# Weight sums issued in the recurrent stage, remainder sums in an earlier phase, the last output pair in pieces

## The chip, the cores and the metric

The kernel runs on one core of a Trainium2 chip. The metric is the device time of one execution, in microseconds (us). The core has a matrix engine (TensorE, PE in the profile), VectorE (DVE), ScalarE (ACT), GpSimd (POOL), and SyncE (SP), which only issues transfers here. POOL issues transfers too. All of them are carried out by the same 16 DMA engines. Each engine works through its instructions in order.

## The reference, cut to what matters

One layer of a streaming encoder, in float32, for 1024 prompt tokens and 32 sample tokens (1056 columns in all), width 1024:

```python
h = rms_norm(x, g_pre_mix)
z = h @ w_in                       # q_A k_A v_A | q_B f_B i_B og_B | gates
ya = sink_attention(...)           # A: 16 heads, window of chunks of 64
yb = hgrn2(...)                    # B: gated linear recurrence, 8 heads of 128
yb = rms_norm(yb) * silu(og_B)
mix = sigmoid(ga) * (ya @ w_br_a) + sigmoid(gb) * (yb @ w_br_b)
x = x + rms_norm(mix @ w_out, g_post_mix)
a, u = split(rms_norm(x) @ w_up)   # 2 x 2816
a = causal_depthwise_conv3(a)
x = x + rms_norm((gelu(a) * u) @ w_down)
x = x + (pe @ w_ple) * sigmoid(x @ w_ple_gate)
```

Beside the tokens it returns the last keys and values, the recurrent state and the last rows ahead of the convolution.

## The kernel before, in words

Every product is made in three: weights and activations are split into a high and a low part, and `product` (L201, L202, L203) multiplies high by high, low by high and high by low. For the large products the kernel uses a Strassen-like scheme with seven block products in place of eight; that needs sums of weight blocks and sums of activation blocks, and sums of the seven results afterwards.

The stages follow one another on PE: the transposed and normed input and attention (A) up to about 402 us; the recurrent stage (B), eight heads; the branches and the output product; the up product; from about 1640 us the down product, in three parts (`seg`) of two phases (`ph`) each; at last the gates and the output.

**Sums of w_down.** The down product needs sums of blocks of `w_down`, for four of its seven products. They are made without an engine: eight sums (`w_sums`), each in four columns, are 32 transfers from DRAM to the DRAM scratch `w_d`, issued by POOL (L1441). 24 read `w_down` and eight read another sum; the transfers that add use the accumulating form. In the program they are traced in the recurrent stage, one every five pieces of work (`at(8 + 5 * (4 * n + c), w_sum)`).

**What sets the order.** A scheduler of the framework places the traced instructions on each engine, and may move one ahead of others traced before it if nothing binds it. `behind(engines)` names the last traced instruction of each of these engines and binds what is traced inside the `with` to come after it; this acts on an instruction of the same engine. The sums are bound to nothing in the kernel before.

**The start.** Input tiles are loaded, transposed and stored to `xt_d` through four buffers `xc` (L775 copies on ACT, L776 stores by SP). Weight columns are loaded to `wr` by SP (L171), and split by ACT (L180, high part `wh`) and DVE (L182, low part `wl`). L339 writes keys into place, L294 stores gates to `ta_d` and `tb_d`. Attention weights `sc` are scaled on DVE (L510) and transposed on PE (L533).

**The recurrent stage.** For each head POOL fills a few tiles, copies `ke` (L1294) and loads the state `S` of the sample (L1315), which DVE uses at L1338. `TL` (L978) and `wu` (L1018) are loads by SP.

**The down product.** `d_unit` runs the products of a column pair `c`, and DVE adds each product's result into accumulators `acc` or into the temporaries `S` and `T`. `rest(c)` (L2251 on) subtracts `S` from `T` (L2255), and adds or subtracts the remainder in three accumulators (L2222). All four calls stand in the second phase of the last part.

**The end.** `gate_one(q, c)` makes the gate product of a quarter `q` and a column pair `c` (both columns `a`) and `y_out` applies tanh and adds; `late_y` turns finished pages back to rows by transposes (L2514, L2526), copies them (L2519, L2520, L2527) and stores them (L2507, L2509, L2531).

Of the kernel before, what the change touches and what calls it, by code (L numbers as in the profile page):

```python
# [10 lines left out]
F32 = mybir.dt.float32  # L11
F32R = mybir.dt.float32r
I32 = mybir.dt.int32
AF = mybir.ActivationFunctionType
ALU = mybir.AluOpType
AX = mybir.AxisListType

P = 128
D = 1024
KT = 8  # L20
# [10 lines left out]
H = 264  # L31
# [28 lines left out]
def layer_kernel(  # L60
# [10 lines left out]
    wp = ctx.enter_context(tc.tile_pool(name="wp", bufs=1, side="left"))  # L71
# [6 lines left out]
    def nm(s):  # L78
        n_names[0] += 1
        return f"{s}_{n_names[0]}"  # L80
# [4 lines left out]
    dma, gdma = nc.sync.dma_start, nc.gpsimd.dma_start  # L85
    V, S, G, E = nc.vector, nc.scalar, nc.gpsimd, nc.tensor

    def behind(*engines):

        st = ExitStack()  # L90
        for e in engines:
            ins = next(i for i in reversed(nc.cur_bb.bb.instructions) if i.engine == e.engine)
            st.enter_context(tc.issue_after(ins))
        return st


    ident = cp.tile([P, P], F32, name="ident")
# [30 lines left out]
    w_d = {o: dp.tile([P, 4, NF // 2, P], F32, name=f"w_d{o}") for o in (1, 3, 4, 6)}  # L128
# [22 lines left out]
    for i in range(8):  # L151
        done, q = sum(G_AT[:i]), [("q", i + 1)] * (3 if i < 7 else 0)
# [86 lines left out]
    def tr_bank():  # L239
        return bank(pp, "tr", 2)  # L240
# [72 lines left out]
    with right("ap") as ap:  # L313
# [91 lines left out]
        qs, biases, yas, probs, o8 = {}, {}, {}, {}, {}  # L405
# [189 lines left out]
        with tc.tile_pool(name="np", bufs=1, side="right", reuse_waits="tile") as np_:  # L595
# [121 lines left out]
            rows = vector_rows()  # L717
# [208 lines left out]
        for i in range(8):  # L926
            lo_ = 2 * len(blocks) if i else 0
            q = unit(q_out(i + 1)) if i < 7 else []
# [148 lines left out]
    with right("bp") as bp:  # L1077
# [309 lines left out]
        pieces, small = [], {}  # L1387
# [49 lines left out]
        for n, (o, a, h, other) in enumerate(w_sums):  # L1437
            for c in range(4):
                def w_sum(o=o, src=w_d[other][:, c] if other else dv[:, a, h, c], c=c,
                          op={"accum_op": ALU.add} if n > 3 else {}):  # L1440
                    gdma(w_d[o][:, c], src, **op)  # L1441
                at(8 + 5 * (4 * n + c), w_sum)
        for m, (run, ev) in enumerate(pieces):
            run()
# [32 lines left out]
    with right("mp") as mp:  # L1477
# [33 lines left out]
        for b_, (c, g) in enumerate(order):  # L1511
            if c == len(ws):
                ws.append(next_w())
            o, n = G4[g]
            ta = mt("ta", 4)
            dma(ta[:], ta_d[c][:, o:o + n])
            b = block(ws[c], ALL, Ra[g], Rb[g], KS, n)
# [25 lines left out]
        for c in range(8):  # L1543
# [3 lines left out]
            for g, (o, n) in enumerate(G4):  # L1547
# [4 lines left out]
                b = block(w, ALL, Ya[g], Yb[g], KS, n)  # L1552
# [321 lines left out]
    for p in range(2):  # L1874
        for c in range(8):
# [14 lines left out]
            if c == 1:  # L1890
# [3 lines left out]
                op0 = build_ops(0)  # L1894
# [16 lines left out]
    t = tr_bank()  # L1911
# [11 lines left out]
    def rows(p):  # L1923
        for h in range(2):
            o, a = H * (2 * p + h), 6 * (1 - p) + 3 * h
            norm_rows(rs[:, a:a + 3], T88, rbT[:, o:o + H])
# [277 lines left out]
    def st_bank():  # L2204
        return pf.tile([P, 2, 512], F32, tag="st", name=nm("st"), bufs=3)
# [45 lines left out]
    def rest(c):  # L2251

        acc = acc_t[c]
        r = S_[:, c]
        V.tensor_tensor(r, T1_[:, c], r, op=ALU.subtract)  # L2255
        add(acc[:, 1], r, ALU.subtract)
        add(acc[:, 3], r)
        add(acc[:, 2], r)
# [26 lines left out]
    def phase_step(pt, ph, s):  # L2285


        if ph == 0:
            a, z_ = range(8), 3
            ops_ = [(pt, 3 + n // 2, n % 2) for n in range(8)]  # L2290
        elif pt < 2:
            a, z_ = range(6), 4
            ops_ = [(pt + 1, n // 2, n % 2) for n in range(6)]
        else:
            return
        if s < len(ops_):
            q, i, p = ops_[s]
            load_op(q, p, i)
        m = s - z_
        if ph:  # L2300
            m = m // 2 if m >= 0 and m % 2 == 0 else -1
        if 0 <= m < len(ops_):
            q, i, p = ops_[m]
            split_ops(q, i, (p,))

    for seg in range(3):
        for ph in range(2):
            if seg == 2 and ph == 1:
                break
            for c in range(4):  # L2310
                def beside(n, c=c):
                    phase_step(seg, ph, len(OPS[ph]) * c + n)
                    if (seg, ph) == (0, 0) and n == 1 and c < 2:
                        with behind(V):
                            next(last_sums)
                d_unit(seg, ph, c, beside=beside)
# [82 lines left out]
    def y_small(n):  # L2399
        return xs_page[0][:, 3].rearrange("p a c -> p (a c)")[:, 256 * (n % 2):256 * (n % 2) + 256]  # L2400
# [3 lines left out]
    for c in range(2):  # L2404
        def beside(n, c=c):
            if n == 0:
                with behind(V):
                    rest(c)
            if n == 1:
                square(c, 0)  # L2410
            if n == 2:
                with behind(S, V):
                    gate_parts(2 * c)
            if n == 3 and c == 0:
                with behind(S, V):
                    gate_parts(1)
        d_unit(2, 1, c, beside=beside)

    def beside(n):
        if n == 0:  # L2420
            with behind(V):
                rest(2)
        if n == 1:
            square(2, 0)
        if n == 2:
            with behind(V):
                rest(3)
        if n == 3:
            square(3, 0)
            xs_page.append(ep.tile([P, 4, 2, H], F32, tag="T1", name="xs"))  # L2430
            for c in range(3):
                x1_load(0, c)
# [27 lines left out]

    d_unit(2, 1, 2, (1,), w2, beside)

    def gate_mults(q, c, b, ks):
        for a in range(2):
            product(b[:, a, :H], gw[2 * c + a], ALL, [xh[q][:, k] for k in range(KT)],
                    [xl[q][:, k] for k in range(KT)], [(k, k) for k in ks], ks[0] == 0, ks[-1] == KT - 1)

    ys, n_pl, n_y = {}, [0], [0]

    def y_out(q, c, b):  # L2470

        p, h = divmod(q, 2)
        if h == 0:
            if not y_pg:
                y_pg.append(page_at(wb_[0], [P, 2, 2, 2 * H], "y").bitcast(F32))
            ys[p, c] = y_pg[0][:, n_y[0] % 2]
            n_y[0] += 1
        y = ys[p, c][:, :, H * h:H * h + H]
        pl = misc[0][:, 2 + n_pl[0] % 2]
        n_pl[0] += 1  # L2480
        dma(pl, ple_d[:, 2 * c:2 * c + 2, H * q:H * q + H])
        ak = columns(q, c)
        for a in (slice(0, 2),) if (q, c) != (3, 3) else (slice(0, 1), slice(1, 2)):
            S.activation(y[:, a], b[:, a, :H], AF.Tanh, scale=0.5)
            V.scalar_tensor_tensor(y[:, a], y[:, a], 1.0, pl[:, a], op0=ALU.add, op1=ALU.mult)
            V.scalar_tensor_tensor(y[:, a], y[:, a], 0.5, ak[:, a], op0=ALU.mult, op1=ALU.add)

    y_pg = []
    TY = (((0, P), (P, P), (2 * P, P), (3 * P, P), (4 * P, 16)),
# [3 lines left out]
    def y_done(p, c):  # L2493

        y = ys.pop((p, c))
        o = 2 * H * p
        fin = (p, c) == (1, 3)
        yr = wp.tile([P, 4, 2 * P], F32, tag="wr", name=nm("yr"), bufs=2)
        sm = y_small(n_done[0])
        n_done[0] += 1  # L2500
        r = TY[p][4][1]
        m3 = TY[p][3][1]

        def rows(z_):
            f = slice(2 * c * P + z_.start, 2 * c * P + z_.stop)
            n = 4 if m3 == P else 3
            dma(y_prompt[0, o:o + n * P, f].rearrange("(a p) c -> p a c", p=P), yr[:, 0:n, z_])  # L2507
            if n == 3:
                dma(y_prompt[0, o + 3 * P:o + 3 * P + m3, f], yr[:m3, 3, z_])  # L2509

        for a in range(2):
            t = tr_bank()
            for i, (c_, m_) in enumerate(TY[p][:4]):
                E.transpose(t[:m_, i * P:(i + 1) * P], y[:, a, c_:c_ + m_], ident[:])  # L2514
            z_ = slice(a * P, (a + 1) * P)
            if m3 == P:
                S.copy(yr[:, :, z_], t[:].rearrange("p (a b) -> p a b", b=P))
            else:
                S.copy(yr[:, 0:3, z_], t[:, :3 * P].rearrange("p (a b) -> p a b", b=P))  # L2519
                S.copy(yr[:m3, 3, z_], t[:m3, 3 * P:])  # L2520
            if fin:
                rows(z_)
        t = tr_bank()
        c_, _ = TY[p][4]
        for a in range(2):
            E.transpose(t[:r, a * P:(a + 1) * P], y[:, a, c_:c_ + r], ident[:])  # L2526
        S.copy(sm[:r], t[:r, :2 * P])  # L2527
        if not fin:
            rows(slice(0, 2 * P))
        f = slice(2 * c * P, (2 * c + 2) * P)  # L2530
        dma(y_sample[0, :, f] if p else y_prompt[0, o + 512:o + 528, f], sm[:r])  # L2531

# [2 lines left out]
    def late_y(n):  # L2535
        while len(late) > n:
            y_done(*late.pop(0))
# [10 lines left out]
    def gate_one(q, c):  # L2548
        b = st_bank()
        gate_mults(q, c, b, tuple(range(KT)))  # L2550
        if q % 2 == 0 or c == 3:
            late_y(1 if q != 3 else 0)
        y_out(q, c, b)
        if q % 2:
            late.append((q // 2, c))
# [25 lines left out]
    for m, (q, c) in enumerate(((0, 2), (1, 2), (0, 3), (1, 3))):  # L2581
        gate_one(q, c)
        for kp in range(2):
            x2_pair(2 + m // 2, 2 * (m % 2) + kp)
    for c in range(4):
        for q in (2, 3):
            gate_one(q, c)
    late_y(0)
    qctx.close()


# [30 lines left out]
```

## Time and profile before

| | us |
|---|---|
| median of 3 runs | 2035.63 (2035.2 to 2039.28) |
| the profiled execution | 2033.22 |
| its span | 2031.4 |
| PE busy | 1951.6 (96%) |
| DVE busy | 1433.0 (71%) |
| ACT busy | 997.8 (49%) |
| POOL busy | 300.7 (15%) |
| mean granted TensorE clock | 0.984 |

In a row of a group the profile gives the source line, the engine, the operation, output and input by the program's names, how often it occurs, and durations. In a row of the timeline stand the start, the duration, the same names, and in square brackets the idle time of the engine ahead of it and what ended that. A row with `SPq` is an issue on SP's queue: its duration is that of the issue, not of the transfer. In a row of windows stand, for each engine, the busy time in that stretch and the number of instructions; then the granted clock (1.00 is full), the mean busy share of the 16 DMA engines (above 1 where more transfers are under way than engines) and what they moved in GB/s.

### The profile page before, as it was taken

What the parts mean: (1) busy time and instruction counts of PE and PEld (TensorE: products, weight loads), DVE (VectorE), ACT (ScalarE), POOL (GpSimd) and SP (SyncE); (2) the same over time, 40 slices, a digit from 0 to 9 for tenths busy, and PEclk for the clock granted to TensorE, in tenths of its full rate; (3) what the DMA queues carried; (4) which work ended last, traced back from release to release, by engine and by line L of the source; (5) the groups of instructions that cost most, each with busy time, mean ns of one, the idle gap of its engine ahead of it and who ended that gap; (6) DMA issues with size and microseconds to landing.
All of it is one profiled execution on the core that took longest, in us unless ns stands there. A gap on an engine that the chain in (4) does not pass through costs nothing. (4 is left out here: it accounts for less than half of the span.)

```text
span 2031.4 us, 38387 instructions
## 1 busy us (share of the span) xinstructions
PE 1951.6 (96%) x14715; PEld 1930.4 (95%) x14715; DVE 1433.0 (71%) x3170; ACT 997.8 (49%) x2181; POOL 300.7 (15%) x423
## 2 busy tenths in 40 slices
PE   5668999999999999999999999999999999999998
PEld 4568999999999999999999999999999999999998
DVE  3346777778888888855355588878787787667872
ACT  4335777766665666645123475333333335534332
POOL 5041212000000000001200123243434320000000
PEclk8789999999999999999999999999999999999999
DMA  9995435231112111148666775333333338555343
GB/s 317 256 204 132 131 90 150 63 131 45 55 57 78 57 54 57 57 139 250 201 187 193 233 242 185 101 106 107 106 107 106 106 113 283 188 182 175 111 128 93
DMA packets 296317, 283.12 MB, mean 139 GB/s; under 512 B 14853, under 2 KB 266376, under 8 KB 296133
## 3 DMA queue, kind: packets, MB, share of 16 engines
q1 hardware_dynamic: 270437, 224.86, 35.7%
q0 software_dynamic: 25696, 55.80, 10.7%
q8 instruction: 116, 1.90, 0.4%
q14 instruction: 68, 0.56, 0.1%
HBM read 195.46 MB, written 100.28 MB: 146 GB/s over the span
## 5 line engine op out<-in xcount | busy, mean ns | idle before, releaser
L2098 PE MATMUL st<-op,wt 128*128 128x264 f32 x1232 | 348.9, 283 | 3.2 <-ACT Sp L2109 1.4
L2100 PE MATMUL st<-op,wt 128*128 128x264 f32 x1232 | 349.7, 284 | 0.0
L2099 PE MATMUL st<-op,wt 128*128 128x264 f32 x1232 | 347.6, 282 | 0.0
L2098 PEld LDWEIGHTS st<-op,wt 128*128 128x128 f32 x1232 | 231.2, 188 | 5.0 <-ACT Sp L2109 2.1
L2099 PEld LDWEIGHTS st<-op,wt 128*128 128x128 f32 x1232 | 231.4, 188 | 0.0
L2100 PEld LDWEIGHTS st<-op,wt 128*128 128x128 f32 x1232 | 230.8, 187 | 0.0
L2217 PE MATMUL st<-dop,wt 128*128 128x264 f32 x616 | 174.8, 284 | 3.3 <-DVE acc L2222 1.9
L2219 PE MATMUL st<-dop,wt 128*128 128x264 f32 x616 | 174.3, 283 | 0.0
L2218 PE MATMUL st<-dop,wt 128*128 128x264 f32 x616 | 174.0, 282 | 0.0
L1762 ACT CAST wt<-wu 128x512 fp32r<-128x512 f32 x126 | 75.9, 618 | 178.1 <-POOL ab L2084 75.5
L201 PE MATMUL mm<-La,wh 128*128 128x384 f32 (+1 forms) x480 | 161.3, 336 | 0.0
L202 PE MATMUL mm<-Lb,wh 128*128 128x384 f32 (+1 forms) x480 | 158.2, 330 | 0.7 <-DVE Lb L771 0.4
L203 PE MATMUL mm<-La,wl 128*128 128x384 f32 (+1 forms) x480 | 157.4, 328 | 0.1
L201 PE MATMUL mm<-Ra,wh 128*128 128x264 f32 x512 | 145.4, 284 | 0.0
L202 PE MATMUL mm<-Rb,wh 128*128 128x264 f32 x512 | 145.0, 283 | 0.0
L203 PE MATMUL mm<-Ra,wl 128*128 128x264 f32 x512 | 145.0, 283 | 0.0
L2217 PEld LDWEIGHTS st<-dop,wt 128*128 128x128 f32 x616 | 115.7, 188 | 4.4 <-ACT wg L2336 1.8
L1763 DVE TENSOR_TENSOR wt<-wu,wt 128x512 fp32r<-128x512 f32 x126 | 86.4, 694 | 46.7 <-ACT wt L1762 46.7
L2218 PEld LDWEIGHTS st<-dop,wt 128*128 128x128 f32 x616 | 115.7, 188 | 0.0
L2219 PEld LDWEIGHTS st<-dop,wt 128*128 128x128 f32 x616 | 115.4, 188 | 0.0
L180 ACT CAST wh<-wr 128x1024 fp32r<-128x1024 f32 x51 | 53.4, 1048 | 97.5 <-PE mm L202 54.1
L202 PEld LDWEIGHTS mm<-Rb,wh 128*128 128x128 f32 x512 | 96.5, 188 | 0.0
(569 smaller groups left out, 6073.8 us busy)
## 6 DMA issues: line engine op xcount, KB each, us to landing
wu<-in_w_up_dram SPq DMA_DIRECT2D x42, 512.0 KB
wu<-in_w_in_dram SPq DMA_DIRECT2D x36, 512.0 KB
w_d<-in_w_down_dram POOLq DMA_DIRECT2D x24, 704.0 KB, 21.3
a_d<-Up SPq DMA_DIRECT2D x22, 528.0 KB
wr<-in_w_in_dram SPq DMA_DIRECT2D x21, 512.0 KB
s_d<-sm SPq DMA_DIRECT2D x40, 264.0 KB
dop<-s_d SPq DMA_DIRECT2D x16, 528.0 KB
wr<-in_w_out_dram SPq DMA_DIRECT2D x16, 512.0 KB
```

The costliest lines, as they stand in the source:

```text
L180: S.copy(hi[:], raw[:])
L201: E.matmul(ps, wh, a, start=first and n == 0, stop=False)
L202: E.matmul(ps, wh, b, start=False, stop=False)
L203: E.matmul(ps, wl, a, start=False, stop=last and n == len(ks) - 1)
L1762: S.copy(t[:, 0], src)
L1763: V.tensor_tensor(t[:, 1], src, t[:, 0].bitcast(F32), op=ALU.subtract)
L2098: E.matmul(o, wh, xh, start=first and k == 0, stop=False, skip_group_check=True)
L2099: E.matmul(o, wh, xl, start=False, stop=False, skip_group_check=True)
L2100: E.matmul(o, wl, xh, start=False, stop=k == 3, skip_group_check=True)
L2217: E.matmul(o, wh, xh_, start=first and k == 0, stop=False, skip_group_check=True)
L2218: E.matmul(o, wh, xl_, start=False, stop=False, skip_group_check=True)
L2219: E.matmul(o, wl, xh_, start=False, stop=k == ng - 1, skip_group_check=True)
```

## The change

There are three edits. First, the 32 transfers of the sums are traced inside `with behind(E, V, G)`. Second, `rest(0)` and `rest(1)` are called in the first phase of the last part (columns 2 and 3, second product), and `rest(2)` and `rest(3)` in the second phase at columns 0 and 1. Third, the last output pair (quarter 3, columns 3) is made in pieces: the two columns' products apart, the first two tiles of the page turned and stored between them, the other three tiles per column, the last column's tanh in pieces of 120 and 144, one copy on DVE, and one store issued by ACT.

```diff
                 def w_sum(o=o, src=w_d[other][:, c] if other else dv[:, a, h, c], c=c,
                           op={"accum_op": ALU.add} if n > 3 else {}):
-                    gdma(w_d[o][:, c], src, **op)
+                    with behind(E, V, G):
+                        gdma(w_d[o][:, c], src, **op)
                 at(8 + 5 * (4 * n + c), w_sum)
...
                 def beside(n, c=c):
                     phase_step(seg, ph, len(OPS[ph]) * c + n)
+                    if (seg, ph, n) == (2, 0, 1) and c > 1:
+                        with behind(V):
+                            rest(c - 2)
...
             if n == 0:
                 with behind(V):
-                    rest(c)
+                    rest(c + 2)
...
     def beside(n):
-        if n == 0:
-            with behind(V):
-                rest(2)
         if n == 1:
             square(2, 0)
-        if n == 2:
-            with behind(V):
-                rest(3)
...
-        if q % 2 == 0 or c == 3:
-            late_y(1 if q != 3 else 0)
+        if q % 2 == 0:
+            late_y(1 if (q, c) != (2, 3) else 0)
...
-    for c in range(4):
-        for q in (2, 3):
-            gate_one(q, c)
-    late_y(0)
+    for q, c in ((2, 0), (3, 0), (2, 1), (3, 1), (2, 2), (3, 2), (2, 3)):
+        gate_one(q, c)
+
+    b = st_bank()
+    ks = tuple(range(KT))
+    gate_mults(3, 3, b, ks, (0,))
+    y = ys[1, 3]
+    yr = wp.tile([P, 4, 2 * P], F32, tag="wr", name=nm("yr"), bufs=2)
+    t = tr_bank()
+    for i in range(2):
+        for a in range(2):
+            o = (2 * i + a) * P
+            E.transpose(t[:, o:o + P], y[:, a, i * P:(i + 1) * P], ident[:])
+    S.copy(yr[:, 0:2].rearrange("p a c -> p (a c)"), t[:])
+    o = 2 * H
+    dma(y_prompt[0, o:o + 2 * P, 6 * P:8 * P].rearrange("(a p) c -> p a c", p=P), yr[:, 0:2])
+    one = slice(0, 1), slice(0, H)
+    piece = y_out(3, 3, b, (one,))
+    gate_mults(3, 3, b, ks, (1,))
...
+    t = tr_bank()
+    for i in (2, 3, 4):
+        last_turn(0, t, i)
+    for i in (2, 3, 4):
+        last_rows(0, t, i, dma)
+    z1, z2 = slice(0, 3 * P - H), slice(3 * P - H, H)
+    t = tr_bank()
+    piece(slice(1, 2), z1)
+    last_turn(1, t, 2)
+    piece(slice(1, 2), z2)
+    last_turn(1, t, 3)
+    last_turn(1, t, 4)
+    for i, q in ((2, dma), (3, S.dma_start), (4, dma)):
+        last_rows(1, t, i, q)
```

In the program as it is placed on the engines, POOL's instructions near the start of the kernel before are these (`w_d_...` are the scratch tensors of the sums, `K...` the keys, `x...` an input tile):

```order
L694 AFFINE_SELECT cm<-cm 128x128
L699 DMA nsink<-in_attn_sinks_dram 128x16
L1441 DMA w_d_144<-in_w_down_dram 128x11x128
L718 COPY tb_185<-tb 32x128
L1441 DMA w_d_144<-in_w_down_dram 128x11x128 x3
L601 MEMSET x_435 32x1024
L602 MEMSET x_435 64x1024
L1441 DMA w_d_145<-in_w_down_dram 128x11x128 x4
L1441 DMA w_d_143<-in_w_down_dram 128x11x128 x4
L1441 DMA w_d_146<-in_w_down_dram 128x11x128 x4
L413 MEMSET qa_1011 128x64
```

None of the sums stands there in the changed kernel. Its first ones on POOL come after the first fills of the recurrent stage, and the others among the heads' instructions:

```order
L1087 MEMSET resets 128x6
L1090 MEMSET z_4929 128x128
L1442 DMA w_d_144<-in_w_down_dram 128x11x128 x2
L1245 MEMSET tq_5027 128x96
L1442 DMA w_d_144<-in_w_down_dram 128x11x128 x2
L1442 DMA w_d_145<-in_w_down_dram 128x11x128
L1245 MEMSET d_933_5325 128x96
L1294 COPY ke_5326<-vt_5242 128x32
L1245 MEMSET tq_5521 128x96
L1442 DMA w_d_145<-in_w_down_dram 128x11x128
L1442 DMA w_d_143<-in_w_down_dram 128x11x128
L1302 MEMSET kk_5633 32x128
```

So the sums moved past all of POOL's attention work. In the last heads the sums that read another sum stand ahead of a head's state load:

```order
L1442 DMA w_d_143<-w_d_145 128x1408
L1442 DMA w_d_146<-w_d_143 128x1408
L1302 MEMSET kk_8522 32x128
L1303 MEMSET kk_8522 64x128
L1442 DMA w_d_143<-w_d_145 128x1408
L1315 DMA S_8741<-in_state_hgrn_dram 128x128
L1442 DMA w_d_143<-w_d_145 128x1408
L1245 MEMSET d_1534_8887 128x96
L1294 COPY ke_8888<-vt_8768 128x32
```

There the load of `S` and the copy `ke` now have sums ahead of them. On DVE, in the last part of the down product, `rest` (the subtraction into `S` and three additions with `S`) stands in the second phase in the kernel before, between the additions of that phase's results `st`:

```order
L2222 TENSOR_TENSOR acc_20038<-acc_20038,st_22222 128x528
L2255 TENSOR_TENSOR S_20039<-T_20035,S_20039 128x528
L2222 TENSOR_TENSOR sq_22081<-sq_22081 128x528
L2222 TENSOR_TENSOR acc_20038<-acc_20038,S_20039 128x528 x3
L2222 TENSOR_TENSOR acc_20038<-acc_20038,st_22223 128x528
L1870 TENSOR_TENSOR wt_22328<-wd_22256,wt_22328 128x512
```

In the changed kernel two of the four groups stand in the first phase, where DVE also prepares operands (`dop`) and weights (`wt`):

```order
L2223 TENSOR_TENSOR T_20035<-T_20035,st_21886 128x528
L2073 TENSOR_TENSOR dop_21846<-dop_21846 128x1056
L2256 TENSOR_TENSOR S_20039<-T_20035,S_20039 128x528
L1871 TENSOR_TENSOR wt_22023<-wd_21919,wt_22023 128x512
L2223 TENSOR_TENSOR acc_20037<-acc_20037,S_20039 128x528 x3
L2223 TENSOR_TENSOR acc_20036<-acc_20036,st_21885 128x528
L2073 TENSOR_TENSOR dop_21881<-dop_21881 128x1056
```

So these two groups moved ahead of the second phase altogether. The other two now follow the first results of its first two columns.

More of the change, by code (lines that the diff above doesn't have):

```diff
@@ L2461, in layer_kernel, with gate_mults @@
     d_unit(2, 1, 2, (1,), w2, beside)
-    def gate_mults(q, c, b, ks):
-        for a in range(2):
+    def gate_mults(q, c, b, ks, cols=range(2)):
+        for a in cols:
             product(b[:, a, :H], gw[2 * c + a], ALL, [xh[q][:, k] for k in range(KT)],
@@ L2468, in layer_kernel, with y_out @@
     ys, n_pl, n_y = {}, [0], [0]
-    def y_out(q, c, b):
+    def y_out(q, c, b, pieces=((slice(0, 2), slice(0, H)),)):
         p, h = divmod(q, 2)
@@ L2482, in y_out, with piece @@
         ak = columns(q, c)
[L2483 to L2486, printed above, removed]
+        def piece(a, z_):
+            S.activation(y[:, a, z_], b[:, a, z_], AF.Tanh, scale=0.5)
+            V.scalar_tensor_tensor(y[:, a, z_], y[:, a, z_], 1.0, pl[:, a, z_], op0=ALU.add, op1=ALU.mult)
+            V.scalar_tensor_tensor(y[:, a, z_], y[:, a, z_], 0.5, ak[:, a, z_], op0=ALU.mult, op1=ALU.add)
+        for z_ in pieces:
+            piece(*z_)
+        return piece
     y_pg = []
@@ L2496, in y_done @@
         o = 2 * H * p
-        fin = (p, c) == (1, 3)
         yr = wp.tile([P, 4, 2 * P], F32, tag="wr", name=nm("yr"), bufs=2)
@@ L2520, in y_done @@
                 S.copy(yr[:m3, 3, z_], t[:m3, 3 * P:])
-            if fin:
-                rows(z_)
         t = tr_bank()
@@ L2527, in y_done @@
         S.copy(sm[:r], t[:r, :2 * P])
-        if not fin:
-            rows(slice(0, 2 * P))
+        rows(slice(0, 2 * P))
         f = slice(2 * c * P, (2 * c + 2) * P)
@@ L2584, in layer_kernel, with last_rows, last_turn @@
             x2_pair(2 + m // 2, 2 * (m % 2) + kp)
-    for c in range(4):
-        for q in (2, 3):
-            gate_one(q, c)
-    late_y(0)
+    for q, c in ((2, 0), (3, 0), (2, 1), (3, 1), (2, 2), (3, 2), (2, 3)):
[16 more added lines that the diff above has]
+    gate_mults(3, 3, b, ks, (1,))
+    sm = y_small(n_done[0])
+    def last_rows(a, t, i, qs):
+        c_, m_ = TY[1][i]
+        z_, f = slice(a * P, (a + 1) * P), slice((6 + a) * P, (7 + a) * P)
+        if i < 4:
+            (V.tensor_copy if i == 3 else S.copy)(yr[:m_, i, z_], t[:m_, i * P - 2 * P:i * P - P])
+            qs(y_prompt[0, o + c_:o + c_ + m_, f], yr[:m_, i, z_])
+        else:
+            S.copy(sm[:m_, z_], t[:m_, 2 * P:3 * P])
+            qs(y_sample[0, :, f], sm[:m_, z_])
+    def last_turn(a, t, i):
+        c_, m_ = TY[1][i]
+        E.transpose(t[:m_, i * P - 2 * P:i * P - P], y[:, a, c_:c_ + m_], ident[:])
+    t = tr_bank()
[12 more added lines that the diff above has]
+        last_rows(1, t, i, q)
     qctx.close()
```

## The prediction

> **What bounds the kernel now.** I read the slices of the span first, then a table of windows over the start, then the waits there, and last single rows.
>
> ```profile
> PE   5668999999999999999999999999999999999998
> DMA  9995435231112111148666775333333338555343
> ```
>
> Each digit is a fortieth of the span, some 51 us. TensorE (PE) is full from the fifth slice to the last one, so what can be won in the middle is small. It is not full in the first four, and there the DMA engines are. The table of windows cuts these four into stretches.
>
> ```profile
> core 0: us, PE busy (x) PEld busy (x) DVE busy (x) ACT busy (x) POOL busy (x), PEclk, DMA share, GB/s
> 0.00:26.00 26.00, 21.57 (x111) 19.03 (x112) 14.57 (x31) 17.10 (x31) 18.61 (x33) 1.00 0.97 333
> 26.00:67.00 41.00, 10.33 (x37) 8.49 (x35) 4.24 (x10) 5.66 (x12) 14.26 (x12) 0.58 1.05 296
> 67.00:108.00 41.00, 35.60 (x218) 33.01 (x218) 24.78 (x66) 22.18 (x46) 8.26 (x17) 0.92 0.91 220
> 108.00:172.00 64.00, 39.49 (x240) 36.93 (x239) 26.17 (x75) 21.88 (x65) 16.27 (x26) 0.84 1.16 218
> 172.00:400.00 228.00, 227.38 (x1598) 225.36 (x1596) 171.59 (x560) 168.38 (x463) 36.83 (x111) 1.00 0.38 104
> ```
>
> From 172 us on, PE idles 0.6 us in 228. Before that it idles 4.4 + 30.7 + 5.4 + 24.5 = 65.0 us, and no other engine is nearly full either: DVE is busy 24.78 of 41 us at most. Only the DMA share stands at 0.91 to 1.16. Whose transfers these are, the rows of the sums' destination `w_d` tell (number, nanoseconds each at least, in the middle and at most, first and last start).
>
> ```profile
> L1441 POOL DMA_DIRECT2D w_d<-in_w_down_dram x24: 1049/1055/3485, 10.5 to 112.8; - x24
> L1441 POOL DMA_DIRECT2D w_d<-w_d x8: 802/812/845, 124.7 to 155.1; - x8
> L1858 SPq DMA_DIRECT2D wd<-w_d x48: 320/430/1227, 1645.8 to 1880.6; - x48
> DMA to landing us min/median/max: 7.7/18.3/42.2
> w_d<-in_w_down_dram POOLq DMA_DIRECT2D x24, 704.0 KB, 21.3
> ```
>
> All 32 are issued by 155.1 us, though nothing reads them before 1645.8. At 704 KB each they are 23.1 MB. The windows moved 8.7 + 12.1 + 9.0 + 14.0 = 43.8 MB up to 172 us, so the sums are half of it. The waits of that stretch (total, times, longest, in us) and the rows of the long ones:
>
> ```profile
> ACT xc L775 <- DMA xt_d<-xc: 36.3, 4, 17.6
> ACT wh L180 <- DMA wr<-in_w_in_dram: 29.2, 2, 22.1
> 47.06 1.65 PE L302 MATMUL tr<-ident,n 128*128 128x128 f32 x6 [14.38 <-ACT xc L775]
> 64.47 0.90 PE L644 MATMUL tr<-ident,x 128*128 128x128 f32 x3 [13.85 <-ACT xc L775]
> 128.41 2.12 SPq L171 DMA_DIRECT2D wr<-in_w_in_dram  x2
> 130.62 19.54 SPq L294 DMA_DIRECT2D ta_d<-gt  x1
> 153.72 1.04 ACT L180 CAST wh<-wr 128x1024 fp32r<-128x1024 f32 x1 [22.09 <-DMA wr<-in_w_in_dram]
> 156.64 1.14 PE L533 MATMUL tr<-ident,sc 128*128 128x128 f32 x4 [19.45 <-DVE sc L510]
> ```
>
> Twice ACT cannot fill a buffer `xc` because its store to `xt_d` has not left, and PE behind it stands 14.38 and 13.85 us. Once a weight load issued at 128.41 is there only at 153.72, 25 us later, and ACT, DVE and PE wait in turn (19.45 us of PE). The SP row of 19.54 us is one issue: SP's queue is held up as well. These transfers stand in one pool with the sums.
>
> **The change part by part, A: the sums.** Their order on POOL moves from the start to behind the first fills of the recurrent stage, which begins near 402 us; PE, DVE, ACT and SP keep their order up to the last part of the down product. Gone from the start are 23.1 MB, 24 issues of 1.05 us at the least and eight of 0.81. What remains there is 20.7 MB. If the 172 us shrink to 117, that is 177 GB/s, against the 333 that the first window reached; so the rest need not bound the start.
>
> The gain, stretch by stretch. In 26 to 67, the idle time is 30.7 us, of which the two `xc` waits are 28.2. The clock was 0.58 there:
>
> ```profile
> 26.12 0.33 PE L202 MATMUL mm<-Lb,wh 128*128 128x384 f32 x1
> 48.82 0.52 PE L202 MATMUL mm<-Lb,wh 128*128 128x384 f32 x1
> ```
>
> The same matmul took 0.52 us behind the wait and 0.33 ahead of it; without the idle time 10.33 us of work become 6.6, 3.8 us less. I take 29 of these 34.5 us, since a store must still leave its buffer. In 67 to 108 I take 4 of the 5.4 idle. In 108 to 172 the 19.45 are due to the late load; the rest of that stretch's idle time is 5.1 us, most of it in pieces that belong to the attention's own chain, and the clock of 0.84 costs some 2 us more. I take 21. Of the first window, 1. Sum: 29 + 4 + 21 + 1 = 55 us. Bounds: at the most everything, 65 + 3.8 + 2 = 70; at the least half of it, 28, if other transfers take the place of the sums, as below.
>
> What the sums cost in their new place. The rows there:
>
> ```profile
> 400.00:500.00 100.00, 99.17 (x654) 98.16 (x654) 79.28 (x169) 61.61 (x132) 2.03 (x11) 1.00 0.29 94
> 500.00:550.00 50.00, 50.00 (x339) 49.82 (x338) 42.88 (x127) 31.26 (x86) 1.65 (x6) 1.00 0.19 58
> 700.00:750.00 50.00, 50.00 (x337) 49.84 (x337) 42.12 (x117) 33.84 (x91) 1.36 (x5) 1.00 0.15 41
> 465.04 0.36 POOL L1294 COPY ke<-vt 128x32 f32<-128x32 f32 x1 [62.05 <-DVE d L1248]
> 504.49 0.57 POOL L1315 DMA_DIRECT2D S<-in_state_hgrn_dram  x1 [21.11 <-PE so L1360]
> 508.48 0.33 DVE L1338 SCALAR_TENSOR_TENSOR S<-S,dec,so 128x128 f32<-128x128 f32 x1
> 418.82 2.78 SPq L978 DMA_DIRECT2D TL<-t_d  x4
> ```
>
> POOL is busy 2 us in 50 and idles 62 us at a stretch, and the DMA share is 0.15 to 0.29: 23.1 MB over some 350 us add 66 GB/s to 41 to 94. PE, though, is full, so what is late there costs directly. Queued behind the sums on POOL are the copy `ke`, two fills and the state's load `S` of each head. `S` is used 4.0 us after its issue. A sum right ahead of it puts it back by an issue (1.05 us) and by its share of the transfer (704 KB at 333 GB/s are 2.2 us), together 3.3 us, which just fits. The first five sums, 3.6 MB or 10.8 us, are issued from 402 and are through near 413, ahead of the four `TL` loads at 418.82. I take a cost of 2 us; bounds 0 (all of it fits) and 16 (eight heads, 2 us each).
>
> A rule stands against this place. The Trainium skill, page "SBUF — State Buffer", section "SBUF: two separate sides", says that a DMA issued by GpSimd has its descriptors written by GpSimd, which some VectorE operations lock out, so the transfer starves. No row of before shows it. By the rule alone each issue would be longer in a stage with DVE at 0.85; even at the longest issue of a sum above (3.49 us) POOL's idle time holds all 32, so my sum stays.
>
> **B: the remainder sums.** Four groups of DVE work move from the second phase of the down product's last part; two of them into its first phase, and the other two from the third column to the first two columns.
>
> ```profile
> 1850.00:1880.00 30.00, 30.00 (x250) 30.00 (x250) 24.77 (x33) 12.14 (x18) 0.00 (x0) 1.00 0.41 123
> 1880.00:1910.00 30.00, 28.01 (x230) 27.29 (x229) 27.08 (x51) 11.95 (x21) 0.00 (x0) 1.00 0.39 116
> 1898.71 0.70 DVE L2255 TENSOR_TENSOR S<-T,S 128x528 f32<-128x528 f32 x1
> 1899.68 1.94 DVE L2222 TENSOR_TENSOR acc<-acc,S 128x528 f32<-128x528 f32 x3
> 1902.72 0.36 PE L2217 MATMUL st<-dop,wt 128*128 128x264 f32 x1 [1.63 <-DVE acc L2222]
> ```
>
> One group is 0.70 + 1.94 = 2.6 us. PE idles 2.0 us in 1880 to 1910, 1.63 of it behind such a group. In the first phase DVE has 5.2 us free in 30, and PE none: two groups, 5.3 us, just fit there. I take a gain of 1.5; bounds 2.0, and a loss of 1.5 if the first phase has DVE late by half of what moves.
>
> **C: the last output pair.** Rows of PE and SP at the end:
>
> ```profile
> 2023.03 0.28 PE L203 MATMUL st<-xh,wg 128*128 128x264 f32 x1
> 2023.15 1.04 PE L2514 MATMUL tr<-ident,y 128*128 128x128 f32 x8
> 2025.15 1.09 PE L2514 MATMUL tr<-ident,y 128*128 128x128 f32 x8 [0.15 <-ACT yr L2520]
> 2028.67 0.39 SPq L2531 DMA_DIRECT2D out_dram<-xs  x1
> ```
>
> Today PE's last product ends at 2023.3; 20 transposes, the copies and eight stores follow, and the span ends at 2031.4, 2.7 us after the last issue. In the change 14 of these transposes (ten of the page before the last, four of the last) stand ahead of the last column's products. A group of eight is 1.04 us; so 14 put the last product back by 1.8 us, to 2025.1. Behind it come six transposes, and shorter pieces: tanh, two DVE operations, a transpose, a copy and the last issue, which I put near 2028.2. Gain 0.5 us; bounds +1 and -1.5 (all of the 1.8 kept but for 0.3).
>
> **The sum.** 55 - 2 + 1.5 + 0.5 = 55 us. The profiled execution took 2033.22 us (span 2031.4 and 1.8 around it) and would take 2033.2 - 55 = 1978.2. The median of the runs, 2035.63, lies 2.4 above it, so I forecast 1980.6. Its own range: 28 to 70 us of A make 1966 to 2008.
>
> **The rivals.**
>
> *The start has a second limit.* Half of the bytes stay, and so does the chain load, split, product; SP still issues one transfer after another, and a store may hold `xc` for long anyway. For it: the first window moved 333 GB/s with PE at 21.57 of 26. Against it: the two rows of `xc` are at 296 GB/s, when sums were most of what flowed. Price: 28 in place of 55, so 2035.6 - 28 = 2007.6. Chance 0.12.
>
> *The recurrent stage gives some back.* `S`, `TL` or `wu` come late behind bursts. It decides where a wait is over the 4.0 us that `S` has. Price: 16 in place of 2: 1994.6. For it: PE has no idle time there. Against it: a DMA share of 0.15 to 0.29. Chance 0.08.
>
> *The wait isn't the sums'.* If each queue of transfers had its share of the engines whatever the other holds, SP's load of 512 KB would be through in twice its 1.6 us at 333 GB/s, not in 25; then the 25 are SP's own queue's (19.54 us for one issue), and the start stays. Left are B and C: 2035.6 - 2.0 = 2033.6, within 0.2%. Against it: SP's own bytes alone can't fill a share of 1.16. Chance 0.03. The Trainium skill, page "DMA: Bandwidth & Descriptors", section "Queues, rings and completion order", has this rule: each DMA engine takes the queues that hold work in turn, a packet at a time. The 25 us of the trace don't look like an even share of bytes.
>
> *Slower: POOL's queue stalls each head.* A sum that waits for a sum (the last eight do: `w_d<-w_d` follow each other every 4.3 us on the mean, and one transfer in the middle lands after 18.3 us) holds the copy `ke` and the load `S` behind it, and PE with them. It decides where a head loses over 57 / 8 = 7.1 us; at 18.3 us less the 4.0 us of slack for each of eight heads it is 114, and 2035.6 - 57 + 114 = 2093. Against it: only in the last two heads do such sums stand ahead of `S`; those ahead of the others read the weights alone. Chance 0.03.
>
> **How the numbers follow.** What a measurement of this kernel can tell from no change is 0.2%, 4 us. The forecast has 0.74, the rivals 0.12, 0.08, 0.03 and 0.03. Faster: 0.74 + 0.12 + 0.08 = 0.94; same 0.03; slower 0.03. The range, 1966 to 2006, leaves out the two last rivals, half of the first and some 0.06 beyond A's upper bound, 0.18 in all.
>
> **What would show it.** In the start no PE wait of over 5 us behind `xc` or `wr`, a clock near 1 in 26 to 67 us, and the stage that begins at 402 us beginning near 347; in the recurrent stage PE full in each window of 50 us while the DMA share rises by some 0.2; behind 1880 us no PE wait of 1.6 us for `acc`; and a last issue under 5.5 us behind the last product. I am wrong if waits for `wr` or `xc` of 10 us remain, or if DVE and PE wait for `S`.

## The result, and the profile after

The changed kernel takes 1962.04 us (median of four runs, 1960.3 to 1962.71), against 2035.41 us before on the same chip: a ratio of 0.9637, with a 95% interval of 0.9619 to 0.9655, some 73 us. I had forecast 1980.6 and a range of 1966 to 2006. The direction was right, the gain was a third larger than forecast, and the time lies 4 us below the range.

The slices of the span after:

```profile
span 1960.9 us, 38386 instructions
PE   8999999999999999999999999999999999999998
DMA  8533433434549531477558582333323347655443
```

PE is full from the second slice on. Much of the DMA engines' load has left the first four slices; the sums are now issued from 331.9 to 724.0 us, the seventh to the fifteenth slice. The table of windows over the start:

```profile
core 0: us, PE busy (x) PEld busy (x) DVE busy (x) ACT busy (x) POOL busy (x), PEclk, DMA share, GB/s
0.00:26.00 26.00, 19.97 (x114) 17.12 (x114) 15.95 (x38) 18.78 (x35) 10.03 (x25) 1.00 0.94 312
26.00:67.00 41.00, 38.49 (x255) 35.86 (x256) 27.88 (x74) 26.97 (x59) 5.95 (x19) 1.00 0.66 198
67.00:108.00 41.00, 41.00 (x278) 40.16 (x277) 28.43 (x84) 24.89 (x69) 2.74 (x14) 1.00 0.42 123
108.00:172.00 64.00, 64.00 (x449) 63.61 (x448) 51.77 (x166) 48.49 (x129) 13.41 (x35) 1.00 0.36 100
```

In 26 to 67 us PE is busy 38.49 us where it was 10.33, and the clock is full. What remains to be moved there flows at 198 GB/s. The waits of PE from 8 to 331 us, the longest ones (total, times, longest):

```profile
PE tr L302 <- DVE n L624: 1.1, 1, 1.1
PE tr L379 <- DVE Vs L344: 1.1, 1, 1.1
PE tr L533 <- DVE pl L225: 0.9, 3, 0.5
```

No wait that a transfer ends is among PE's, and none is over 1.1 us. To see where the time came off, I compared PE's order in both traces: the k-th matmul of a line before against the k-th of the same line after, start minus start (at the first matmul from the time named on).

```
time before, us    earlier after by, us
26                  0.7
67                 36.2
108                41.8
156                45.2   (ahead of the transposes at 156.64)
157                65.0   (behind them)
175                70.3
401                70.1   (start of the recurrent stage)
1225               70.2
1250               68.0
1700               67.5
1905               70.25
end of the span    70.5
```

All of the gain is there at 175 us. The recurrent stage gives none of it back. 2.2 us go at 1233 to 1241, where some waits are longer than before and the profile's record of the granted clock has a half-speed stretch of 3.4 us; the remainder sums bring 2.7, the last pair some 0.3. The profiled execution of the changed kernel is the longest of its four runs, so the difference of the medians is a little larger than the 70.5 of the two profiles.

### The profile page after: what moved, and what is told of

It reads as the page before. It is cut to its first block, busy times and chain, and to the rows that moved or that the text cites. A ratio compares the mean times of both kernels' runs of the same rounds, so it can differ in the third digit from the quotient of the medians.

```text
span 1960.9 us, 38386 instructions
## 1 busy us (share of the span) xinstructions
PE 1938.8 (99%) x14715; PEld 1921.4 (98%) x14715; DVE 1432.0 (73%) x3174; ACT 997.9 (51%) x2182; POOL 299.7 (15%) x423
## 5 line engine op out<-in xcount | busy, mean ns | idle before, releaser
L201 PEld LDWEIGHTS mm<-Ra,wh 128*128 128x128 f32 x512 | 96.4, 188 | 0.0
```

What stands on the lines that cost most here:

```text
L201: E.matmul(ps, wh, a, start=first and n == 0, stop=False)
```

## The experiments

**Each edit by itself.** The first edit alone, in the kernel before:

```diff
-                    gdma(w_d[o][:, c], src, **op)
+                    with behind(E, V, G):
+                        gdma(w_d[o][:, c], src, **op)
```

> The kernel before with the first edit alone (sums held to the recurrent stage). The traces of before and after put PE's matmuls 70.3 us earlier from 175 us on, and the remainder sums 2.7 us, the last pair 0.3 us earlier. If these prices are the edits' own, this run stands 70 us below before, near 1965, and 3 us above the changed kernel; PE's order times in the recurrent stage equal those of after. If the sums' new place costs the 2 us that I had put on it, it is 1967 or more.

It took 1965.5 us (1964.32 to 1968.49), ratio 0.9662 (0.9646 to 0.9678). PE's order times stand 69.8 us earlier from 175 us on and 69.5 at 475 us. So the first edit is the gain, and its place in the recurrent stage costs nothing that can be seen; it is 3.5 us above the median of the changed kernel.

The other two edits alone, the sums at the start:

> The second and the third edit alone, the sums at the start as before. From the traces of before and after: 2.7 us by the remainder sums and 0.3 by the last pair, so 3 us less than before. My prediction's terms are 1.5 and 0.5. PE's order times ahead of 1680 us are those of before, and behind 1905 us 2.7 us earlier.

It took 2030.05 us (2027.73 to 2037.27), ratio 0.9986 (0.9974 to 0.9999): some 2.8 us, with 0.2 to 5.3 by the interval, about as expected. In its trace PE's order shifts by 2.8 us between 1875 and 1905 us of before, as it does in the changed kernel (2.7). Against what I had expected, its times ahead of that are not those of before: from 1242 us on PE is 4.0 us later, behind a half-speed stretch of 6.8 us that the profile of before doesn't have.

The changed kernel without the third edit, beside the changed kernel:

> The changed kernel without the third edit (the last pair in one piece, as before). My term for that edit is 0.5 us, with -1.5 to 1 as bounds; the traces so far show between -1.1 and 0.3 from the last product's shift to the end of the span. So this run should be within 1 us of the changed kernel, in either direction, which its runs can hardly tell apart; in its trace the stretch from the last gate product to the last store's issue shows the edit's price.

> The changed kernel once more, beside the run without the third edit: 1960 to 1963. A half-speed stretch of the clock near 1168 us, of 3.4 us in the profile of the changed kernel, is absent or up to 7 us long by the execution; with it the time moves by up to 4 us.

1962.5 us (1959.45 to 1963.83) without the third edit, 1963.14 (1961.86 to 1965.55) with it: ratios 0.9643 (0.9617 to 0.9669) and 0.965 (0.9624 to 0.9676). The two can't be told apart. The last store's issue in the four traces with the edit stands where PE's shift alone would put it, within 0.1 us; the end of the span comes 0.3 us earlier in three of them and 1.1 later in one. So the edit is worth nothing that was measured.

**Which sums made which wait.** Only the last eight sums, those that read another sum, are held to the recurrent stage:

```diff
-                          op={"accum_op": ALU.add} if n > 3 else {}):
-                    gdma(w_d[o][:, c], src, **op)
+                          op={"accum_op": ALU.add} if n > 3 else {}, late=n > 5):
+                    with behind(*((E, V, G) if late else ())):
+                        gdma(w_d[o][:, c], src, **op)
```

> The kernel before with only the last eight sums (those that read another sum) held to the recurrent stage; the first 24 stay at the start. If each group of sums makes its own waits, the two waits for xc (14.4 and 13.9 us) stay, the wait of 19.5 us near 137 us goes with the low clock behind it: 24 to 27 us less than before, near 2010. If the waits follow the bytes, a quarter of the sums is a quarter of 70: 18 us, and the wait for the weight load is shortened, not gone. If the wait near 137 us is SP's own, it stays: 2035.

2018.39 us, one run, 15.1 us below the kernel before. The shift is 1.4 us at 125 and 17.6 at 175. The wait near 137 us is shortened and not gone:

```profile
142.84 1.14 PE L533 MATMUL tr<-ident,sc 128*128 128x128 f32 x4 [7.08 <-DVE sc L510]
```

7.08 us are left of 19.45. This is what I had put down to bytes (18 us less), and not the 24 to 27 that I had for sums which each make a wait of their own. The run doesn't settle it: by the packets in its trace, sums of the first 24 are still under way up to some 140 us, and a wait that they share with the last eight is shortened in both theories.

**Bytes or turns.** The view of the DMA queues of the kernel before, in the three stretches of its start: 26 to 60 us (plain sums), 66 to 90 (adding sums that read the weights), 138 to 156 (sums that read another sum). q0 is POOL's queue, q1 SP's; packets, MB, share of 16 engines.

```profile
q0 software_dynamic: 2395, 8.64, 84.4%
q1 hardware_dynamic: 2396, 1.65, 15.6%
...
q1 hardware_dynamic: 3475, 4.50, 57.9%
q0 software_dynamic: 2936, 1.48, 48.8%
...
q0 software_dynamic: 753, 3.51, 95.8%
q1 hardware_dynamic: 751, 0.38, 10.3%
```

In the first and the last stretch the numbers of packets are equal: 2395 and 2396, 753 and 751. There the two queues take turns, one packet each. But the packets are not equal. In the last stretch one of POOL's is 3.51 MB / 753 = 4660 bytes and holds an engine 0.958 x 18 us x 16 / 753 = 366 ns; one of SP's is 506 bytes and 39 ns. So SP has a tenth of the time and moves 0.38 MB in 18 us, 21 GB/s. A load of 512 KB at 21 GB/s takes 25 us, and 25 us is what the load issued at 128.41 took. In the middle stretch the sums' packets are 504 bytes, and SP moves 188 GB/s beside them; there PE hardly waited. That made the theory of turns: the price of a sum isn't its bytes but the size of its packets. The middle stretch alone doesn't prove it, since SP's own packets are 1295 bytes on the mean there and the counts are not equal.

The test keeps every byte and, row for row in the traces, the order of PE, DVE and ACT, and pads the scratch, so that rows of 128 numbers stand apart:

```diff
-    w_d = {o: dp.tile([P, 4, NF // 2, P], F32, name=f"w_d{o}") for o in (1, 3, 4, 6)}
+    w_d = {o: dp.tile([P, 4, NF // 2, 2 * P], F32, name=f"w_d{o}")[:, :, :, 0:P] for o in (1, 3, 4, 6)}
```

> The kernel before, with the order of all engines unchanged, but the scratch of the sums is padded: rows of 128 numbers stand apart, so that a sum that reads another sum moves pieces of 512 bytes in place of rows of 5632. Bytes, issues and places are the same. Theory of turns: its packets shrink from 5000 bytes (390 ns) to some 505 bytes (64 ns), SP gets 35 / (35 + 64) = a third of the engines' time in place of a tenth, and the PE wait of 19.5 us near 137 us shrinks below 9 us: 10 us or more less than before by 175 us, near 2022. If the plain copies also go as small packets, the two waits of 14 us shrink too, to 5 or less each: near 2000. By bytes: the sums take 1.6 times the engine time (64 ns for 505 bytes against 390 for 5000), so the wait stays or grows: 2034 to 2045.

2014.89 us, one run, against 2033.51 of the kernel before on that chip: 18.6 us less, where the theory by bytes had no gain. The queues in 138 to 156 us, the windows, the two waits at `xc`, the wait that was 19.45 us long, and the sums:

```profile
q0 software_dynamic: 3906, 1.98, 86.4%
q1 hardware_dynamic: 2835, 1.75, 44.4%
...
26.00:67.00 41.00, 12.03 (x42) 10.57 (x42) 5.18 (x13) 7.56 (x16) 13.44 (x12) 0.58 1.05 301
108.00:172.00 64.00, 57.67 (x367) 55.45 (x366) 40.51 (x114) 33.85 (x94) 24.67 (x30) 0.95 1.34 208
...
45.24 1.65 PE L302 MATMUL tr<-ident,n 128*128 128x128 f32 x6 [12.17 <-ACT xc L775]
61.50 0.90 PE L644 MATMUL tr<-ident,x 128*128 128x128 f32 x3 [12.68 <-ACT xc L775]
139.87 0.45 PE L533 MATMUL tr<-ident,sc 128*128 128x128 f32 x1 [4.85 <-DVE sc L510]
L1441 POOL DMA_DIRECT2D w_d<-w_d x8: 1849/1863/1877, 122.6 to 165.5; - x8
```

POOL's packets are now 507 bytes, SP moves 1.75 MB in the 18 us in place of 0.38, and PE is busy 57.67 of 64 us where it was 39.49, though the engines' share is higher (1.34 against 1.16), the sums' issues take 1.86 us in place of 0.81, and the sums themselves last 10 us longer. Of the wait of 19.45 us 4.85 are left. The plain sums still go in packets of some 3600 bytes (8.83 MB in 2431 packets from 26 to 60 us), and the two waits that they make stay: 12.17 and 12.68 us. One run holds the effect and its control; whether smaller plain packets would shorten those two as well wasn't tried. POOL's 3906 packets to SP's 2835 are not one to one; whether SP's queue had work all the time there, the view doesn't say.

**Another stage.** The sums are issued one by one through the attention stage, in the kernel before (the list of sums stands ahead of that stage's stream of work):

```diff
-                at(8 + 5 * (4 * n + c), w_sum)
+                small.setdefault(12 + 2 * (4 * n + c), []).append(lambda f=w_sum: pinned(f, E, G))
```

> All 32 sums issued one by one through the attention stage in place of the start, in the same form as before (packets of 4 to 5 KB in before's trace). Theory of turns: the DMA engines take one packet of POOL's queue and one of SP's in turn, so beside packets of 4 KB (160 to 390 ns) SP's 512-byte packets (35 ns) get a tenth of the time; 512 KB then take 15 to 25 us, the weight loads of the attention stage come late, and PE waits there: 20 to 60 us above the kernel with the sums in the recurrent stage, 1985 to 2025. Rival, by bytes: the DMA share in 172 to 400 us is 0.38, the sums add 0.4, it all fits, and PE stays full: 1962 to 1970.

1984.9 us, one run: 19 us above the kernel with the first edit alone (1965.5) and a hair below what the theory of turns had. My sum by bytes was wrong ahead of any theory: the DMA share came to 1.08 in 200 to 250 us, not to 0.8, so the run doesn't tell turns from engines that are simply full. A part of the price is of another kind. In this stage the low parts of weights are made by a transfer of POOL's own queue, and it lands later behind the sums. How the price divides isn't shown. Its landing (least, middle, most), before and here:

```profile
DMA to landing us min/median/max: 4.5/4.9/7.3
```

```profile
DMA to landing us min/median/max: 4.6/10.0/19.6
```

The same places, with each sum's pieces in another order, so that all go in runs of 128 numbers:

> As the run before, at the same places in the program, but each sum is written in runs of 128 numbers (512 bytes), so that its packets are small. Theory of turns: SP's packets wait for 63 ns and not for 200 to 390, a load of 512 KB takes 6 to 7 us, PE waits little: 1965 to 1980, well below the run with large packets. By bytes there is no difference between the two, or the small packets are worse, as they take 63 ns for 505 bytes against 390 for 5000, 60% more engine time for the same bytes. If the plain copies still go as 4 KB packets, only the adding sums, the last half, show the difference.

2122.0 us, one run: far above, and against what I expected. It doesn't count against the turns, and not for them: in its trace some of PE's, DVE's, ACT's and POOL's instructions stand in another order than in the run before; why the scheduler placed them so isn't shown. SP's weight loads made ACT wait here as well, eight times and 41.4 us in all. The longest waits of PE and POOL:

```profile
PE s L496 <- DVE st L502: 60.6, 22, 9.9
```

```profile
POOL qa L413 <- PE s L497: 114.9, 5, 24.6
```

POOL stands for PE, PE for DVE, and DVE for ACT (92.2 us); what begins this chain isn't shown. As a test of packet sizes it failed; the padded scratch, which leaves the order alone, was the better one.

**All at once.** The changed kernel with the sums in one burst at the beginning of the recurrent stage:

```diff
-                at(8 + 5 * (4 * n + c), w_sum)
+                at(8, w_sum)
```

> The changed kernel with all 32 sums issued in one burst at the beginning of the recurrent stage, and not one every five pieces of work. Theory of turns: for some 80 to 100 us SP's loads (TL, wu) get a small share, and POOL's copy ke and its fills stand behind the sums' issues; PE waits 20 to 70 us: 1982 to 2032. By the prices of my prediction (at most 2 us a head, 16 in all): 1981 at the most, and if bytes alone count, 1962 to 1970.

2006.46 us, one run: 44 us above the changed kernel. PE's shift is 70.1 us at 425 us of before and 26.9 at 500, and stays there. The longest wait of ACT in 330 to 480 us, and rows:

```profile
ACT wt L1030 <- DMA wu<-in_w_in_dram: 31.2, 2, 17.1
388.42 0.62 ACT L1030 CAST wt<-wu 128x512 fp32r<-128x512 f32 x1 [14.16 <-DMA wu<-in_w_in_dram]
394.91 0.66 PE L1109 MATMUL Z<-La,wt 128*128 128x384 f32 x1 [13.82 <-DVE tf L1137]
452.50 0.62 ACT L1030 CAST wt<-wu 128x512 fp32r<-128x512 f32 x1 [17.07 <-DMA wu<-in_w_in_dram]
```

It is the start over again: SP's loads of 512 KB come 14 and 17 us late. The queues of this run from 385 to 397 us (adding sums that read the weights) and from 433 to 445 (sums that read another sum):

```profile
q0 software_dynamic: 2381, 1.26, 79.6%
q1 hardware_dynamic: 2359, 1.19, 49.7%
...
q0 software_dynamic: 467, 2.33, 95.2%
q1 hardware_dynamic: 468, 0.24, 9.6%
```

Here the packets are one to one both times, and in both SP's are some 510 bytes. Beside packets of 529 bytes SP moves 99 GB/s, beside packets of 4990 it moves 20. So small packets are not free either, but they leave SP five times as much.

So the recurrent stage isn't safe as such. By these two runs, what made the place free is that a few sums go at a time, with pauses in which SP's loads land. The changed kernel's windows there:

```profile
430.00:480.00 50.00, 50.00 (x338) 49.82 (x338) 42.75 (x126) 31.36 (x86) 6.87 (x11) 1.00 0.47 130
580.00:680.00 100.00, 100.00 (x668) 99.70 (x667) 81.61 (x218) 65.49 (x166) 17.41 (x20) 1.00 0.75 136
```

PE is full at a DMA share of 0.47 and 0.75.

## Why the prediction was right and wrong

**What bounds the start: right.** The waits that I named were the ones that went, and they went with the sums.

**The gain of the start: wrong in size.** The failing steps are "I take 29 of these 34.5 us, since a store must still leave its buffer", "I take 4 of the 5.4 idle" and "I take 21": 55 us with the 1 of the first window. By the shifts above they are 35.5, 5.6, 28.5 and 0.7, together 70.3. The part held back, 15 us, had no row behind it. In the changed kernel's trace a store that must leave its buffer holds PE for 0.7 us at the most, by way of DVE at `xc`. Two rows said so in advance: no engine was near full there, and from 172 us on PE idled 0.6 us in 228 with the same kinds of loads and stores in flow. The other term that was too small is the time in which PE worked slowly, which I put at 3.8 in the first of these stretches and some 2 in the last. Here is the last stretch of before up to 175 us, and behind it the same three stretches of PE's work in the changed kernel:

```profile
108.00:175.00 67.00, 42.49 (x258) 39.90 (x257) 28.44 (x81) 23.77 (x70) 16.27 (x26) 0.85 1.13 215
...
25.33:30.80 5.47, 5.43 (x37) 4.95 (x36) 3.06 (x6) 4.81 (x11) 0.00 (x0) 1.00 0.43 109
30.80:66.25 35.45, 32.95 (x219) 30.57 (x219) 24.82 (x69) 22.77 (x48) 5.95 (x19) 1.00 0.69 211
66.25:104.75 38.50, 38.50 (x258) 37.57 (x257) 26.54 (x80) 22.92 (x64) 2.55 (x13) 1.00 0.45 132
```

PE's busy time falls from 10.33 to 5.43, from 35.60 to 32.95 and from 42.49 to 38.50, together 11.5 us where I had 5.8; with 58.0 us less idle time and the 0.7 of the first window that is the 70. The views don't part the slower clock from the overlap of matmuls that a wait breaks. My upper bound for the first edit, 70, met the value by luck: it took all 65 us of idle time, of which 58.7 came off, and too little for the slow work, and the two errors cancel. The range ended there, with nothing added for the other two edits.

**A likely reason behind the size: I read the share of the queues wrongly.** In "The wait isn't the sums'" I worked out a load's time at an even share of bytes, twice 1.6 us, found that the 25 us don't fit it, and left the rule of turns at that. That this is why I held back 15 us is likely, but the prediction doesn't say so. The turns are there, packet for packet, and it is the packets that are not even. The Trainium skill, page "DMA: Bandwidth & Descriptors", section "Queues, rings and completion order", says that an engine takes the queues in turn a packet at a time; this case's traces agree, with 753 and 751 packets side by side (packets as the profile counts them). Had I asked for the view of the queues and divided the bytes by the packets, the 25 us of the load would have come out of it, and with them that the wait was the sums'. The measurement speaks for the waits being theirs: the padded scratch cut the one to 4.85 us and left the other two.

**The new place: nearly right.** I took a cost of 2 us with bounds of 0 and 16, and the trace shows 0.0. The copy `ke` and the load `S` had the slack that the rows gave them; `S` is used 4.0 us after its issue, as before:

```profile
434.31 0.60 POOL L1315 DMA_DIRECT2D S<-in_state_hgrn_dram  x1 [19.38 <-PE so L1360]
434.90 1.08 POOL L1442 DMA_DIRECT2D w_d<-in_w_down_dram  x1
438.30 0.33 DVE L1338 SCALAR_TENSOR_TENSOR S<-S,dec,so 128x128 f32<-128x128 f32 x1
```

The case that I priced didn't come: ahead of this `S` POOL waits 19.4 us for PE, and the sum before it had been issued 20 us or more earlier in each head. Had it come, the 3.3 us would not have fitted as I wrote, since I left out the 2.1 us that `S` itself takes from issue to landing. And my upper bound of 16 was one for this spacing alone; the burst cost 44. That GpSimd is kept from writing descriptors by VectorE doesn't show: the issue of a sum takes 1.08 us in the middle there, 1.05 at the start before.

```profile
L1442 POOL DMA_DIRECT2D w_d<-in_w_down_dram x24: 1049/1076/3526, 331.9 to 602.7; - x24
```

**The remainder sums: right in kind, too small.** 2.7 us for my 1.5, above my bound of 2.0. I took the idle time that the view shows for all that the waits cost. The matmuls of this product start 0.12 us apart and last 0.28, so they overlap, and a wait costs more than its idle time: ahead of the wait of 1.63 us one starts at 1900.81 and the next at 1902.72, 1.8 us more than usual. Two short breaks near 1896 and 1898 bring the other 0.9, of which the view shows 0.3 as idle. The 0.8 us of idle time in 1910 to 1940 are still there in the changed kernel. In the first phase DVE had the room, as worked out:

```profile
1780.00:1810.00 30.00, 30.00 (x250) 30.00 (x249) 28.00 (x40) 11.20 (x17) 0.00 (x0) 1.00 0.40 120
```

DVE is at 28.00 of 30 us, and PE stays full.

**The last pair: within its bounds.** 0.5 forecast, and nothing measured. The transposes put the last product back by 2.1 us (1.8 forecast), and the way from it to the last issue shrinks from 5.4 to 3.3 us, just as much. The sign that I gave for this edit, a last issue under 5.5 us behind the last product, already held before, so it could show nothing.

**The rivals.** None of them came. What the second one told of, SP's loads late in the recurrent stage, comes in the burst, at 44 us where I had 16.

## What to carry to other kernels

Where two queues of transfers are busy at once, divide bytes by packets for each: SP's loads in packets of some 510 bytes moved 20 GB/s beside packets of 4990 bytes, and 99 GB/s beside packets of 529. The start, where no engine was near full and the long waits ended on transfers, gave up 58.7 of its 65.0 us of PE's idle time and 11.5 us of slow work when the transfers that crowded it went; holding part of such a stretch back needs a row. Move bulk transfers that nobody awaits to where PE is covered, a few at a time: the same 32 transfers cost 70 us at the start, 19 spread over the attention stage, 44 in one burst in the recurrent stage, and nothing spread over that one.

## What the runs showed of the hardware that I had not expected

Transfers from DRAM to DRAM go in packets of different sizes by their form: a plain sum with 512-byte pieces on one side in some 3600 bytes on the mean, an adding one in 505, an adding one over rows of 5632 bytes in 4660 on the mean; padding the rows apart brought the last to 507. The half-speed stretch of the clock near the beginning of the up product was absent, 3.4 or 6.8 us long in the profiles that I compared, behind waits of PE of 0.3 to 2.8 us. With the longer waits ahead of it it cost 2.2 us in the changed kernel's profile and some 4 in three others. The longest of these waits doesn't settle it: it was 1.23 us in the profile of the changed kernel, which has a stretch, and 1.22 in the one of the same kernel once more, which has none. What makes it come stays open; it wasn't tried.
